# Evacuating a PSUM bank behind its last product, loading rows of x ahead, and moving row sums in a one-layer hybrid decoder kernel

## The chip, the cores and the metric

The kernel runs on one core of a Trainium2 chip. The time is device microseconds (us) of one execution of the whole program. TensorE is called PE here, VectorE DVE, ScalarE ACT, GpSimd POOL and SyncE SP; SP issues most of the transfers.

## The reference

One decoder layer in float32 on x with 512 rows and 2048 columns. Two attention groups share an input projection: A is a sliding-window attention with sinks, B a stick-breaking attention. Each group's output is RMS-normalised, both go through one output projection, and a squared-ReLU MLP of width 8192 follows:

```python
proj = rmsnorm(x, g) @ w_in                     # q_a k_a v_a q_b k_b v_b
o_a  = swa_attention(rmsnorm(q_a), rmsnorm(k_a), v_a, sinks, rel_bias)
o_b  = stick_breaking_attention(q_b, k_b, v_b)
mix  = concat([rmsnorm(o_a, swa_out_g), rmsnorm(o_b, sb_out_g)])
x    = x + mix @ w_out
u    = rmsnorm(x, norm_mlp_g) @ w_up
x    = x + square(relu(u)) @ w_down
```

The stick-breaking weights need, for each query, a running sum over the keys to its right (a scan on DVE).

## The kernel before, in words

Every float32 operand of PE is split into a high part (ACT copies it, L91) and a low part (DVE subtracts, L92), and each product is made as three matmuls (`mm3`, L113 to 118). PE's work comes in this order on the timeline of the profile:

- 0 to 140 us: load and transpose x, first projections.
- 140 to 500 us: the remaining input projections, in groups of four PSUM banks (`group_T` at L297 for q and k, `v_group` at L519 for v). Each group walks over the inner dimension in steps c; in each step it makes products into each of its four banks, and after every second bank it calls `pump()` (L276), which puts one step of an attention unit into the stream: scores z of a stick-breaking pair (L547), their weights (L560 to 572, on ACT, DVE and POOL; the scan is L567, the subtraction that reads the scores a last time is L569), and the transposes wtr of the weights (L581).
- 500 to 640 us: the first half of the output projection, `out_group(0, n)` for n of 0 to 3 (L645), on the normalised output of group B. The last stick-breaking pairs are still pumped in.
- 640 to 780 us: the second half, `out_group(1, n)`, with `evac_b` (L716) and the transposes of the new x.
- 780 to 1400 us: the up projection. For each step i, `u_load` (L762) fetches a raw weight tile, `u_sums` (L769) forms four sums of its blocks on POOL (L779), and `u_split` makes high and low parts (hi_u on ACT, lo_u on DVE); PE makes products 128x256 (L809 to 811).
- 1400 to 2041 us: the down projection (L1053 to 1055). Its weights are raw tiles (st_d) and differences of them, called T1 to T4, made on POOL by `d_sum` (L931), in two halves each; T1 of the first column is issued within the last steps of the up projection (k == 4 there).

PSUM has two pools of four banks: `pp` holds the banks of projections (ps_qk, ps_v, ps_o), `pa` scores, transposes and the sums of squares. A new tile takes the bank that comes next in rotation and waits for the last reader of what was there. Within an engine, instructions run in the order in which the program's framework places them; that order follows the order of the code with small shifts by which instruction is ready.

In the code before, a group evacuates its four banks after the loop over c: `group_T` by `evac` (L319, DVE), `v_group` by L535 on ACT, `out_group` by `evac_a` or `evac_b`. `evac_a` (L675) takes a buffer xs (tag "bias", two buffers), asks SP for 128 rows of x, adds them to the scaled bank on DVE (L678), and stores the sum. `branch_scale(b)` (L634) sums the squares S of a branch on PE with a vector of ones (rs, L637) and makes the branch's scale rb from it; `branch_scale(0)` stands before the first `out_group(0, 0)`, `branch_scale(1)` before `out_group(1, 0)`.

## Time and profile before

| quantity | value |
|---|---|
| runs | 2041.43, 2043.79 and 2044.12 us, median 2043.79 |
| profiled execution | 2043.11 us, its span 2041.0 |
| PE busy | 2004.0 us, 98% |
| DVE busy | 1626.8 us, 80% |
| POOL busy | 1020.3 us, 50% |
| ACT busy | 1014.5 us, 50% |
| DMA queue of the hardware | 345.02 MB, 49.8% of 16 engines |

The span runs from the first to the last recorded instruction; the profiled execution is 2.1 us longer. Busy time is summed over instructions, so idle time of PE is what is left, and for each idle stretch the trace names the instruction whose end released it. A granted clock of 1 means TensorE's full 2.4 GHz, 0.5 means 1.2 GHz.

### The profile page before, as it was taken

How to read it: one execution, taken by the hardware profiler on the slowest of the kernel's cores; microseconds unless marked ns; L12 is line 12 of the kernel's file. 1: busy time of each engine (PE TensorE's matmuls, PEld its weight loads, DVE VectorE, ACT ScalarE, POOL GpSimd, SP SyncE). 2: the span in 40 equal slices, each digit the busy share in tenths (PEclk: the TensorE clock that was granted, in tenths of full speed). 3: DMA queues.
4: the chain of work that ended last, by engine and by line, in shares of the span. 5: the costliest groups of instructions: out<-in, count | busy, mean ns of one | idle time of the engine just before them, and what ended most of it. 6: DMA issues, size and time to landing. Idle time of an engine off the chain costs nothing. (4 is left out here: it accounts for less than half of the span.)

```text
span 2041.0 us, 31132 instructions
## 1 busy us (share of the span) xinstructions
PE 2004.0 (98%) x11748; PEld 1725.3 (85%) x11748; DVE 1626.8 (80%) x2034; ACT 1014.5 (50%) x1676; POOL 1020.3 (50%) x904
## 2 busy tenths in 40 slices
PE   8999999999999999999999999998999999999998
PEld 7887787778677889999999999997788888888887
DVE  4378646665775578999999999998989999999987
ACT  6267534544553565555555555554543333333343
POOL 0014332222320127777777777775756556655654
PEclk9999999999999999999999999999999999999999
DMA  6742332223345555665656565656756557456351
GB/s 220 123 129 85 100 93 81 73 92 111 107 134 186 168 166 182 203 203 183 203 182 205 182 205 182 206 182 264 273 223 227 177 216 267 155 226 258 145 186 62
DMA packets 213914, 350.30 MB, mean 172 GB/s; under 512 B 9779, under 2 KB 154372, under 8 KB 206596
## 3 DMA queue, kind: packets, MB, share of 16 engines
q1 hardware_dynamic: 211216, 345.02, 49.8%
q10 hardware_dynamic: 2548, 3.30, 1.3%
q8 instruction: 92, 1.51, 0.3%
q14 instruction: 58, 0.48, 0.1%
HBM read 270.16 MB, written 78.12 MB: 171 GB/s over the span
## 5 line engine op out<-in xcount | busy, mean ns | idle before, releaser
L811 PE MATMUL ps_u<-h2h,lo_u 128*128 128x256 f32 x1824 | 515.9, 283 | 6.3 <-DVE lo_u L92 6.3
L810 PE MATMUL ps_u<-h2l,hi_u 128*128 128x256 f32 x1824 | 514.7, 282 | 2.4 <-DVE h2l L92 2.4
L809 PE MATMUL ps_u<-h2h,hi_u 128*128 128x256 f32 x1824 | 514.8, 282 | 0.1
L1053 PE MATMUL ps_d<-hi_d,ad 128*128 128x512 f32 x896 | 353.4, 394 | 3.4 <-ACT U L969 1.6
L1054 PE MATMUL ps_d<-lo_d,ad 128*128 128x512 f32 x896 | 353.4, 394 | 1.2 <-DVE lo_d L92 1.2
L1055 PE MATMUL ps_d<-hi_d,ad 128*128 128x512 f32 x896 | 353.2, 394 | 0.0
L811 PEld LDWEIGHTS ps_u<-h2h,lo_u 128*128 128x128 f32 x1824 | 346.7, 190 | 7.5 <-DVE lo_u L92 6.7
L810 PEld LDWEIGHTS ps_u<-h2l,hi_u 128*128 128x128 f32 x1824 | 346.6, 190 | 2.9 <-DVE h2l L92 2.8
L809 PEld LDWEIGHTS ps_u<-h2h,hi_u 128*128 128x128 f32 x1824 | 346.6, 190 | 0.3 <-ACT h2h L91 0.3
L779 POOL TENSOR_TENSOR s_u<-st_u 128x256 f32<-128x256 f32 (+1 forms) x256 | 200.1, 801 | 252.3 <-DVE lo_u L92 181.2
L92 DVE TENSOR_TENSOR lo_d<-T,hi_d 128x1024 fp32r<-128x1024 f32 x128 | 241.4, 1899 | 38.1 <-ACT hi_d L91 37.4
L931 POOL TENSOR_TENSOR T<-st_d,T 128x1024 f32<-128x1024 f32 x64 | 169.1, 2645 | 201.0 <-DVE lo_d L92 198.5
L91 ACT CAST hi_d<-T 128x1024 fp32r<-128x1024 f32 x128 | 134.4, 1051 | 203.0 <-PE ps_d L1055 177.6
L92 DVE TENSOR_TENSOR lo_u<-st_u,hi_u 128x384 fp32r<-128x384 f32 (+1 forms) x256 | 218.2, 853 | 4.4 <-ACT hi_u L91 4.3
L1053 PEld LDWEIGHTS ps_d<-hi_d,ad 128*128 128x128 f32 x896 | 167.9, 187 | 44.6 <-ACT U L969 2.1
L92 DVE TENSOR_TENSOR lo_d<-st_d,hi_d 128x1024 fp32r<-128x1024 f32 x96 | 193.5, 2028 | 13.7 <-ACT hi_d L91 13.2
L1054 PEld LDWEIGHTS ps_d<-lo_d,ad 128*128 128x128 f32 x896 | 168.0, 188 | 42.0 <-DVE lo_d L92 2.0
L1055 PEld LDWEIGHTS ps_d<-hi_d,ad 128*128 128x128 f32 x896 | 168.0, 187 | 40.1
L92 DVE TENSOR_TENSOR lo_u<-s_u,hi_u 128x512 fp32r<-128x512 f32 x224 | 178.1, 795 | 1.0 <-ACT hi_u L91 1.0
L91 ACT CAST hi_u<-s_u 128x512 fp32r<-128x512 f32 x224 | 138.5, 618 | 78.7 <-POOL s_u L779 78.6
L91 ACT CAST hi_d<-st_d 128x1024 fp32r<-128x1024 f32 x96 | 100.6, 1050 | 152.2 <-PE ps_d L1055 140.6
L779 POOL TENSOR_TENSOR s_u<-st_u,s_u 128x256 f32<-128x256 f32 (+1 forms) x128 | 167.8, 1311 | 10.0
(223 smaller groups left out, 3825.7 us busy)
## 6 DMA issues: line engine op xcount, KB each, us to landing
st_u<-in_w_up SPq DMA_DIRECT2D x128, 512.0 KB, 4.5
st_d<-in_w_down SPq DMA_DIRECT2D x64, 1024.0 KB, 8.3
ad<-ac SPq DMA_DIRECT2D x56, 1024.0 KB, 5.1
ac<-ah SPq DMA_DIRECT2D x32, 896.0 KB, 6.3
ac<-al SPq DMA_DIRECT2D x32, 896.0 KB, 6.6
st_qk<-in_w_in SPq DMA_DIRECT2D x64, 256.0 KB, 3.0
st_o<-in_w_out SPq DMA_DIRECT2D x32, 512.0 KB, 4.5
st_qa<-in_w_in SPq DMA_DIRECT2D x16, 512.0 KB, 4.1
```

Source lines behind the costliest of these rows:

```text
L91: nc.scalar.copy(out=hi, in_=st)
L92: nc.vector.tensor_tensor(out=lo, in0=st, in1=hi.bitcast(F32), op=ALU.subtract)
L779: nc.gpsimd.tensor_tensor(out=o, in0=a, in1=b, op=op)
L809: nc.tensor.matmul(o, wh[:, a], hh[:, b], start=first, stop=False, skip_group_check=True)
L810: nc.tensor.matmul(o, wh[:, a], hl[:, b], start=False, stop=False, skip_group_check=True)
L811: nc.tensor.matmul(o, wl[:, a], hh[:, b], start=False, stop=(k == KP - 1), skip_group_check=True)
L931: nc.gpsimd.tensor_tensor(out=o, in0=raw[cj, a, h], in1=raw[cj, b, h], op=ALU.subtract)
L1053: nc.tensor.matmul(o, al, bh[:, kk], start=first, stop=False, skip_group_check=True)
L1054: nc.tensor.matmul(o, al, bl[:, kk], start=False, stop=False, skip_group_check=True)
L1055: nc.tensor.matmul(o, ar, bh[:, kk], start=False, stop=end, skip_group_check=True)
```

## The change

Six things move. `group_T`, `v_group` and `out_group` call the evacuation directly behind a bank's last product, inside the loop. The rows of x for `evac_a` are asked for in step c2 == 2 of their group, into four buffers instead of two. `branch_scale(0)` moves into `out_group(0, 0)`, behind the second bank of step 1. `branch_scale(1)`, the end of the attention pools and the opening of the pools h2, sp and xw move into step 1 of `out_group(1, 0)`. T1 of the first column of the down projection is placed behind the last of the sums of w_up on POOL. A padding tile becomes 24 columns wide instead of 32. No engine gets another set of instructions.

```diff
     def group_T(src, name, evac, perm=None, after=None):
-        ps = [pp.tile([P, 512], F32, tag="pp", name=f"ps_{name}{m}") for m in range(4)]
+        ps, done = [pp.tile([P, 512], F32, tag="pp", name=f"ps_{name}{m}") for m in range(4)], []
...
                     mm3(ps[m], (hi[:, kk, ms], lo[:, kk, ms]), (hT[k][:, 0], hT[k][:, 1]),
                         k == 0, k == KD - 1)
+                if c == KD // 2 - 1:
+                    done.append(evac(m, ps[m]))
                 if m % 2:
                     pump()
             if after:
                 after(c)
-        return [evac(m, ps[m]) for m in range(4)]
+        return done
...
-    const.tile([P, 32], F32, name="pad_left")
+    const.tile([P, 24], F32, name="pad_left")
...
-            bias.append(wk.tile([P, 2, 2 * P], F32, tag="bias", name=f"bias{c}"))
+            bias.append(wk.tile([P, 2, 2 * P], F32, tag="bias", bufs=4, name=f"bias{c}"))
...
     def v_group(o):
...
+                if c == KD // 2 - 1:
+                    v = vp.tile([P, 512], F32, tag="v", name=f"v{o}_{t}")
+                    nc.scalar.mul(out=v, in_=ps[t], mul=r1[:, t:t + 1])
+                    vs.append(v)
                 if t % 2:
                     pump()
-        vs = []
-        for t in range(NT):
-            v = vp.tile([P, 512], F32, tag="v", name=f"v{o}_{t}")
-            nc.scalar.mul(out=v, in_=ps[t], mul=r1[:, t:t + 1])
-            vs.append(v)
         return vs
...
-    def out_group(b, n, evac, ahead=None, between=None):
+    def out_group(b, n, evac, ahead=None, between=None, within=None):
...
                     mm3(ps[t], (oc[:, 0, ts], oc[:, 1, ts]), (hi[:, kk], lo[:, kk]), c == 0, c == 7)
+                if c2 == 3:
+                    evac(n, t, ps[t])
                 if t % 2:
                     pump()
+                if within and (c2, t) == (1, 1):
+                    within()
             if between and c2 in (1, 2):
                 between(c2 - 1)
-        for t in range(NT):
-            evac(n, t, ps[t])
...
-    ra = branch_scale(0)
+    rs, xs_of = {}, {}
 
     def evac_a(n, t, ps):
-        xs = wk.tile([P, 512], F32, tag="bias", name=f"xs{n}{t}")
-        nc.sync.dma_start(out=xs, in_=xv[:, t, n * 512:(n + 1) * 512])
-        nc.vector.scalar_tensor_tensor(out=xs, in0=ps, scalar=ra[:, t:t + 1], in1=xs, op0=ALU.mult, op1=ALU.add)
+        xs = xs_of.pop(t)
+        nc.vector.scalar_tensor_tensor(out=xs, in0=ps, scalar=rs[0][:, t:t + 1], in1=xs, op0=ALU.mult, op1=ALU.add)
         nc.sync.dma_start(out=ascr[n, :, t], in_=xs)
 
+    def ahead_a(n, fetching):
+        def ahead(c2):
+            if fetching:
+                fetching(c2)
+            if c2 == 2:
+                for t in range(NT):
+                    xs_of[t] = wk.tile([P, 512], F32, tag="bias", bufs=4, name=f"xs{n}{t}")
+                    nc.sync.dma_start(out=xs_of[t], in_=xv[:, t, n * 512:(n + 1) * 512])
+        return ahead
+
+    def scale_a():
+        rs[0] = branch_scale(0)
+
     for n in range(4):
-        out_group(0, n, evac_a, fetch_two(0) if n == 0 else fetch_two(1) if n == 3 else None)
+        out_group(0, n, evac_a, within=scale_a if n == 0 else None, ahead=ahead_a(n, fetch_two(0) if n == 0 else fetch_two(1) if n == 3 else None))
     drain()
-    rb_ = branch_scale(1)
-    attn.close()
     even.close()
...
+    def begin_b(c2):
+
+        if c2 == 1:
+            rs[1] = branch_scale(1)
+            attn.close()
+            for k in range(6):
+                hp.append(mlp.enter_context(tc.tile_pool(name=f"h2_{k}", bufs=1, side="right")))
+            pools["sp"] = mlp.enter_context(tc.tile_pool(name="sp", bufs=2, side="right"))
+            pools["xw"] = tail.enter_context(tc.tile_pool(name="xw", bufs=4, side="right"))
...
-                nc.gpsimd.tensor_tensor(out=o, in0=a, in1=b, op=op)
+                last_sum[0] = nc.gpsimd.tensor_tensor(out=o, in0=a, in1=b, op=op)
...
-        out_group(1, n, evac_b, ahead=u_begin if n == 3 else None,
+        out_group(1, n, evac_b, ahead={0: begin_b, 3: u_begin}.get(n),
...
                 elif k == 4:
-                    d_sum(0, "T1")
+                    with tc.issue_after(last_sum[0].ins):
+                        d_sum(0, "T1")
```

What moves on the engines is shown at three places, the first on two engines. The rows name the output, the inputs and the shape; line numbers behind the change are larger by 2 to 22, since the file has grown.

The first is PE at the start of the first output projection. ps_o001 is the second bank of the first group, hi_o and lo_o are parts of w_out, rs0 is the sum of squares, z4_30 and z4_31 are the scores of the last block of a stick-breaking pair. Before:

```order
L116 MATMUL ps_o001_4939<-hi_o000_4944,ohl0_0_4565 128x512
L637 MATMUL rs0_4923<-ones2_494,S0_585 128x2 x4
L117 MATMUL ps_o001_4939<-lo_o000_4945,ohl0_0_4565 128x512
L118 MATMUL ps_o001_4939<-hi_o000_4944,ohl0_0_4565 128x512
L116 MATMUL ps_o001_4939<-hi_o000_4944,ohl0_1_4601 128x512
L117 MATMUL ps_o001_4939<-lo_o000_4945,ohl0_1_4601 128x512
L118 MATMUL ps_o001_4939<-hi_o000_4944,ohl0_1_4601 128x512
L547 MATMUL z4_30_4960<-hl_b22_4489,hl_b20_4479 128x512
L547 MATMUL z4_31_4961<-hl_b22_4489,hl_b20_4479 128x512
```

Behind the change, at the same place:

```order
L116 MATMUL ps_o001_4924<-hi_o000_4929,ohl0_0_4565 128x512
L117 MATMUL ps_o001_4924<-lo_o000_4930,ohl0_0_4565 128x512
L118 MATMUL ps_o001_4924<-hi_o000_4929,ohl0_0_4565 128x512
L116 MATMUL ps_o001_4924<-hi_o000_4929,ohl0_1_4601 128x512
L117 MATMUL ps_o001_4924<-lo_o000_4930,ohl0_1_4601 128x512
L118 MATMUL ps_o001_4924<-hi_o000_4929,ohl0_1_4601 128x512
L549 MATMUL z4_30_4945<-hl_b22_4483,hl_b20_4461 128x512
L549 MATMUL z4_31_4946<-hl_b22_4483,hl_b20_4461 128x512
```

rs0 has left this place, so z4_30 is the first here that takes a bank of the pool `pa`. rs0 stands one step later, behind the first scores of the next pair (z5_00 and z5_01) and ahead of the third bank:

```order
L549 MATMUL z5_00_5019<-hl_b23_4494,hl_b21_4472 128x256
L549 MATMUL z5_01_5020<-hl_b23_4494,hl_b21_4472 128x256
L639 MATMUL rs0_5053<-ones2_494,S0_585 128x2 x4
L116 MATMUL ps_o002_4925<-hi_o001_5003,ohl0_2_4637 128x512
L117 MATMUL ps_o002_4925<-lo_o001_5004,ohl0_2_4637 128x512
```

Here rs0 takes the bank behind those of z5_00 and z5_01.

On DVE at the same time, f_b is the evacuation of the last bank of a q and k group (ps_qk_3), and b4_20, a4_20, b4_21, a4_21 are the two chains of one pair whose scores lie in the banks that PE takes next. Before:

```order
L563 SCALAR_TENSOR_TENSOR b4_20_4852<-z4_20_4843,a4_20_4851 128x384
L563 SCALAR_TENSOR_TENSOR b4_21_4865<-z4_21_4844,a4_21_4864 128x384
L567 SCALAR_TENSOR_TENSOR a4_20_4851<-ones2_494,b4_20_4852 128x384
L567 SCALAR_TENSOR_TENSOR a4_21_4864<-ones2_494,b4_21_4865 128x384
L569 TENSOR_TENSOR b4_20_4852<-z4_20_4843,a4_20_4851 128x384
L569 TENSOR_TENSOR b4_21_4865<-z4_21_4844,a4_21_4864 128x384
L582 COPY wt4_0_4811<-wtr4_10_4889 128x2x128
L582 COPY wt4_1_4812<-wtr4_11_4893 128x2x128
L319 SCALAR_TENSOR_TENSOR f_b33_4917<-ps_qk3_3_4500,rbc_514 128x512
```

Behind the change:

```order
L565 SCALAR_TENSOR_TENSOR b4_20_4862<-z4_20_4853,a4_20_4861 128x384
L321 SCALAR_TENSOR_TENSOR f_b33_4904<-ps_qk3_3_4500,rbc_514 128x512
L569 SCALAR_TENSOR_TENSOR a4_20_4861<-ones2_494,b4_20_4862 128x384
L565 SCALAR_TENSOR_TENSOR b4_21_4875<-z4_21_4854,a4_21_4874 128x384
L571 TENSOR_TENSOR b4_20_4862<-z4_20_4853,a4_20_4861 128x384
L569 SCALAR_TENSOR_TENSOR a4_21_4874<-ones2_494,b4_21_4875 128x384
L584 COPY wt4_0_4811<-wtr4_10_4909 128x2x128
L571 TENSOR_TENSOR b4_21_4875<-z4_21_4854,a4_21_4874 128x384
```

The evacuation has moved from behind the chains to between them, and the first chain's subtraction (L571) now stands ahead of the second chain's scan (L569).

The second is DVE at the end of the first group of that projection, where xs are the evacuations and b_20, b_21 belong to the third block of a pair's weights. Before:

```order
L678 SCALAR_TENSOR_TENSOR xs00_5256<-ps_o000_4938,rb0_4928,xs00_5256 128x512
L678 SCALAR_TENSOR_TENSOR xs01_5260<-ps_o001_4939,rb0_4928,xs01_5260 128x512
L563 SCALAR_TENSOR_TENSOR b5_20_5211<-z5_20_5202,a5_20_5210 128x384
L563 SCALAR_TENSOR_TENSOR b5_21_5224<-z5_21_5203,a5_21_5223 128x384
L567 SCALAR_TENSOR_TENSOR a5_20_5210<-ones2_494,b5_20_5211 128x384
L567 SCALAR_TENSOR_TENSOR a5_21_5223<-ones2_494,b5_21_5224 128x384
L569 TENSOR_TENSOR b5_20_5211<-z5_20_5202,a5_20_5210 128x384
L569 TENSOR_TENSOR b5_21_5224<-z5_21_5203,a5_21_5223 128x384
L582 COPY wt5_0_5171<-wtr5_10_5248 128x2x128
L582 COPY wt5_1_5172<-wtr5_11_5252 128x2x128
L92 TENSOR_TENSOR lo_o013_5516<-st_o013_5513,hi_o013_5515 128x1024
L678 SCALAR_TENSOR_TENSOR xs02_5264<-ps_o002_4940,rb0_4928,xs02_5264 128x512
```

Behind the change:

```order
L681 SCALAR_TENSOR_TENSOR xs00_5113<-ps_o000_4923,rb0_5058,xs00_5113 128x512
L681 SCALAR_TENSOR_TENSOR xs01_5115<-ps_o001_4924,rb0_5058,xs01_5115 128x512
L681 SCALAR_TENSOR_TENSOR xs02_5117<-ps_o002_4925,rb0_5058,xs02_5117 128x512
L565 SCALAR_TENSOR_TENSOR b5_20_5223<-z5_20_5214,a5_20_5222 128x384
L565 SCALAR_TENSOR_TENSOR b5_21_5236<-z5_21_5215,a5_21_5235 128x384
L569 SCALAR_TENSOR_TENSOR a5_20_5222<-ones2_494,b5_20_5223 128x384
L569 SCALAR_TENSOR_TENSOR a5_21_5235<-ones2_494,b5_21_5236 128x384
L571 TENSOR_TENSOR b5_20_5223<-z5_20_5214,a5_20_5222 128x384
L571 TENSOR_TENSOR b5_21_5236<-z5_21_5215,a5_21_5235 128x384
L681 SCALAR_TENSOR_TENSOR xs03_5119<-ps_o003_4926,rb0_5058,xs03_5119 128x512
L584 COPY wt5_0_5179<-wtr5_10_5264 128x2x128
```

Three evacuations stand ahead of the chain of the next block where there were two, and the fourth stands directly behind it.

The third is POOL at the end of the up projection; s_u126 and s_u127 are the last sums of w_up, T1_00 and T1_01 the two halves of T1, st_d raw tiles of w_down. Before:

```order
L779 TENSOR_TENSOR s_u125_15371<-st_u125_15236,s_u125_15371 128x2x128
L931 TENSOR_TENSOR T1_00_15576<-st_d000_15477 128x1024
L779 TENSOR_TENSOR s_u126_15440<-st_u126_15303 128x2x128 x2
L779 TENSOR_TENSOR s_u126_15440<-s_u126_15440,st_u126_15303 128x2x128
L779 TENSOR_TENSOR s_u126_15440<-st_u126_15303,s_u126_15440 128x2x128
L931 TENSOR_TENSOR T1_01_15578<-st_d001_15479 128x1024
L779 TENSOR_TENSOR s_u127_15511<-st_u127_15369 128x128 x2
L779 TENSOR_TENSOR s_u127_15511<-s_u127_15511,st_u127_15369 128x128
L779 TENSOR_TENSOR s_u127_15511<-st_u127_15369,s_u127_15511 128x128
L931 TENSOR_TENSOR T3_00_15731<-st_d010_15713,st_d000_15477 128x1024
```

Behind the change:

```order
L801 TENSOR_TENSOR s_u125_15371<-st_u125_15236,s_u125_15371 128x2x128
L801 TENSOR_TENSOR s_u126_15440<-st_u126_15303 128x2x128 x2
L801 TENSOR_TENSOR s_u126_15440<-s_u126_15440,st_u126_15303 128x2x128
L801 TENSOR_TENSOR s_u126_15440<-st_u126_15303,s_u126_15440 128x2x128
L801 TENSOR_TENSOR s_u127_15511<-st_u127_15369 128x128 x2
L801 TENSOR_TENSOR s_u127_15511<-s_u127_15511,st_u127_15369 128x128
L801 TENSOR_TENSOR s_u127_15511<-st_u127_15369,s_u127_15511 128x128
L953 TENSOR_TENSOR T1_00_15576<-st_d000_15477 128x1024
L953 TENSOR_TENSOR T1_01_15578<-st_d001_15479 128x1024
L953 TENSOR_TENSOR T3_00_15731<-st_d010_15713,st_d000_15477 128x1024
```

The two halves of T1 have moved from between the sums to behind the last one.

## Rows read from the trace of the kernel before

**Rows 1.** Page, part 1: busy us (share of the span) and instructions of each engine.

```profile
PE 2004.0 (98%) x11748; PEld 1725.3 (85%) x11748; DVE 1626.8 (80%) x2034; ACT 1014.5 (50%) x1676; POOL 1020.3 (50%) x904
```

**Rows 2.** Waits of PE: line, releaser, us in total, times, longest.

```profile
PE ps_u L811 <- DVE lo_u L92: 6.3, 2, 5.4
...
PE ps_o L116 <- DVE xs L678: 4.2, 4, 1.5
...
PE wtr L581 <- ACT b L572: 2.5, 2, 1.6
...
PE z L547 <- DVE b L569: 1.2, 2, 0.6
```

**Rows 3.** Timeline of PE at 515 us: start, us, instruction [idle before, releaser].

```profile
515.86 1.05 PE L637 MATMUL rs<-ones,S 128*128 128x2 f32 x8 [3.08 <-DVE b L569]
```

**Rows 4.** Windows: length, busy of PE, PEld, DVE, ACT, POOL, clock, DMA, GB/s.

```profile
500.00:540.00 40.00, 35.99 (x178) 26.27 (x177) 28.57 (x46) 21.49 (x50) 13.29 (x21) 0.96 0.25 77
...
1398.80:1404.40 5.60, 5.60 (x26) 5.60 (x27) 4.37 (x5) 4.25 (x4) 2.38 (x1) 0.50 0.29 100
```

**Rows 5.** Timeline of PE at 619 us.

```profile
619.05 0.50 PE L116 MATMUL ps_o<-hi_o,ohl 128*128 128x512 f32 x1 [1.49 <-DVE xs L678]
```

**Rows 6.** The evacuations of L678: durations, and what DVE waited for.

```profile
L678 DVE SCALAR_TENSOR_TENSOR xs<-ps_o,rb,xs x16: 737/744/752, 545.6 to 651.8; 128x512 f32<-128x512 f32 x16
...
  DMA xs<-in_x: 5.4, 6
```

**Rows 7.** Timeline of DVE at 559 us.

```profile
559.47 1.26 DVE L569 TENSOR_TENSOR b<-z,a 128x512 f32<-128x512 f32 x2
```

**Rows 8.** Timeline of PE at 560 us.

```profile
559.93 0.39 PE L117 MATMUL ps_o<-lo_o,ohl 128*128 128x512 f32 x1
560.16 0.39 PE L118 MATMUL ps_o<-hi_o,ohl 128*128 128x512 f32 x1
560.48 0.63 PE L547 MATMUL z<-hl_b,hl_b 64*128 64x256 f32 x6
```

**Rows 9.** Timeline of DVE from 509 to 516 us.

```profile
509.39 0.69 DVE L319 SCALAR_TENSOR_TENSOR f_b<-ps_qk,rbc 128x512 f32<-128x512 f32 x1 [0.21 <-PE ps_qk L118]
...
511.16 4.19 DVE L567 TENSOR_TENSOR_SCAN a<-ones,b 128x384 f32<-128x384 f32 x2
515.28 0.99 DVE L569 TENSOR_TENSOR b<-z,a 128x384 f32<-128x384 f32 x2
```

**Rows 10.** Timeline of POOL at 511 us.

```profile
511.12 1.30 POOL L315 TENSOR_TENSOR hl_b<-f_b,hl_b 128x512 fp32r<-128x512 f32 x1
```

**Rows 11.** Timeline of DVE at 613 us, scans of that form.

```profile
613.59 2.04 DVE L567 TENSOR_TENSOR_SCAN a<-ones,b 128x384 f32<-128x384 f32 x2
```

**Rows 12.** Timeline of PE, end of the up projection.

```profile
1398.73 0.58 PE L811 MATMUL ps_u<-h2h,lo_u 128*128 128x256 f32 x1 [5.40 <-DVE lo_u L92]
```

**Rows 13.** Timeline of POOL, end of the up projection.

```profile
1378.11 2.78 POOL L931 TENSOR_TENSOR T<-st_d 128x1024 f32<-128x1024 f32 x1 [1.57 <-DVE lo_u L92]
...
1385.25 2.38 POOL L931 TENSOR_TENSOR T<-st_d 128x1024 f32<-128x1024 f32 x1
...
1390.44 2.86 POOL L931 TENSOR_TENSOR T<-st_d,st_d 128x1024 f32<-128x1024 f32 x1
1393.26 2.53 POOL L931 TENSOR_TENSOR T<-st_d,T 128x1024 f32<-128x1024 f32 x1
1395.75 2.52 POOL L931 TENSOR_TENSOR T<-st_d,st_d 128x1024 f32<-128x1024 f32 x1
```

**Rows 14.** Timeline of DVE, end of the up projection.

```profile
1391.92 1.67 DVE L836 TENSOR_TENSOR a<-a 128x256 f32<-128x256 f32 x1 [0.89 <-ACT a L834]
1393.51 2.56 DVE L839 TENSOR_TENSOR a<-a 128x256 f32<-128x256 f32 x1
1395.99 2.69 DVE L92 TENSOR_TENSOR lo_u<-st_u,hi_u 128x384 fp32r<-128x384 f32 x1
...
1399.65 0.42 DVE L840 TENSOR_TENSOR a<-a 128x256 f32<-128x256 f32 x1
```

More of the change, by code (lines that the diff above doesn't have):

```diff
@@ L521, in v_group @@
         src = cols(w_in, O5 + 512 * o)
+        vs = []
         for c in range(KD // 2):
@@ L707, in hymba_layer @@
     tail = ExitStack()
-    for k in range(6):
-        hp.append(mlp.enter_context(tc.tile_pool(name=f"h2_{k}", bufs=1, side="right")))
-    sp = mlp.enter_context(tc.tile_pool(name="sp", bufs=2, side="right"))
-    xw = tail.enter_context(tc.tile_pool(name="xw", bufs=4, side="right"))
+    pools = {}
+    def begin_b(c2):
[6 more added lines that the diff above has]
+            pools["xw"] = tail.enter_context(tc.tile_pool(name="xw", bufs=4, side="right"))
     h2 = {}
@@ L716, in evac_b @@
     def evac_b(n, t, ps):
-        xt = xw.tile([P, 512], F32, tag="xt", name=f"x2_{n}{t}")
+        xt = pools["xw"].tile([P, 512], F32, tag="xt", name=f"x2_{n}{t}")
         nc.sync.dma_start(out=xt, in_=ascr[n, :, t])
-        nc.vector.scalar_tensor_tensor(out=xt, in0=ps, scalar=rb_[:, t:t + 1], in1=xt, op0=ALU.mult, op1=ALU.add)
+        nc.vector.scalar_tensor_tensor(out=xt, in0=ps, scalar=rs[1][:, t:t + 1], in1=xt, op0=ALU.mult, op1=ALU.add)
         nc.sync.dma_start(out=x2scr[n, :, t], in_=xt)
-        xs = xw.tile([P, 512], F32, tag="xs", bufs=8, name=f"xs2_{n}{t}")
+        xs = pools["xw"].tile([P, 512], F32, tag="xs", bufs=8, name=f"xs2_{n}{t}")
         nc.scalar.activation(out=xs, in_=xt, func=AF.Square, accum_out=ss2[:, t, n:n + 1])
@@ L739, in turn_x2 @@
         k = 2 * n + kk
-        hq = xw.tile([P, 8, HP], F32, tag="hq", bufs=1, name=f"hq{k}")
+        hq = pools["xw"].tile([P, 8, HP], F32, tag="hq", bufs=1, name=f"hq{k}")
         for r in range(2):
@@ L759, in hymba_layer @@
     wu = w_up.rearrange("(k p) c -> p k c", p=P)
-    raws, sums, parts_u = {}, {}, {}
+    raws, sums, parts_u, last_sum = {}, {}, {}, [None]
     def u_load(i):
@@ L771, in u_sums @@
             w = raws[i]
-            s_ = sp.tile([P, 2, 4, P], F32, tag="s", name=f"s_u{i}")
+            s_ = pools["sp"].tile([P, 2, 4, P], F32, tag="s", name=f"s_u{i}")
             if i % (KP // 2) == PLAIN // 2:
```

## The prediction

> **What bounds the kernel now.** I read the busy shares of the page first: PE is busy for 2004.0 of 2041.0 us [rows 1]. The change removes no product, so it can win idle time of PE or time at the low TensorE clock, nothing else. Next I read the list of what PE waited for [rows 2]. Five of its lines lie where the change moves something: the banks of the first out projection that wait for their evacuation on DVE (L678), 4.2 us in four waits; the transposes of the stick-breaking weights (wtr, L581) that wait for ACT, 2.5 in two; the low parts of w_up at the end of the up projection (lo_u, L92), 6.3 in two; and the scores z, 1.2 in two; the row sums of squares (rs, L637) are the fifth, one wait of 3.08 [rows 3]. Third, the windows [rows 4]. In 500 to 540 us the granted clock is 0.96 of full speed (600 to 640, around the longest xs wait, has the same 0.96), and 40 x 0.04 = 1.6 us of full-speed work is lost in each; from 1398.8 to 1404.4 it is 0.50, that is 1.2 instead of 2.4 GHz, so 5.6 x 0.5 = 2.8 us are lost. Last, the timelines around each wait; they come with the parts below.
>
> The bound is therefore PE in order, and each gap stands for one late tile of another engine.
>
> **First out projection, evacuations (xs).** The longest of the four waits is the 1.49 us in front of 619.05 [rows 5]: the next group's first product needs a bank that DVE has not read yet. One evacuation takes 0.744 us, sixteen of them together waited 5.4 us for x rows still in flight [rows 6], because the old code asks for a row when it evacuates. The change asks for the four rows half a group earlier and evacuates a bank behind its last product, while PE still has up to three banks of six products to make. Both causes go, so 4.2 us is the upper end of the gain. What is late next are the scores: DVE now does three evacuations ahead of the next pair's weights where it did two, and that chain gives back the two banks that the next scores take. Its last subtractions run to 559.47 + 1.26 = 560.73, and PE starts the next scores at 560.48 [rows 7, 8]: no slack for one more evacuation of 0.744. The nearest price is the z line of [rows 2], 0.6 each; I take two of them, 1.2, with ends of 0 and 4.2 (every wait moves from xs to z). Net **3.0**.
>
> **Sums of squares later (rs0).** Before, PE stands 3.08 us in front of 515.86 because rs0 takes the bank of a score whose subtraction on DVE (L569) is late [rows 3]. DVE is late since its two scans took 4.19 us [rows 9], while POOL subtracted in SBUF at 511.12 [rows 10]; the same two scans elsewhere take 2.04 [rows 11]. Moving rs0 does not free a bank: z4_30 and z4_31 now take that bank and the next one. PE arrives five products later, 5 x 0.23 = 1.15 us (two products in a row start at 559.93 and 560.16 [rows 8]). The second bank needs the second subtraction, half of 0.99 later, and DVE's order now has an evacuation of 0.69 between the two chains [rows 9]. With scans as slow as before the wait is 3.08 - 1.15 + 0.50 + 0.69 = 3.1, no gain; with scans at 2.04 it is 2.15 less, 1.0. The gain lies between 0 and 2.1; I take the middle, **1.0**. In its new place rs0 stands behind the scores z5_0 and takes whichever bank is next; its 8 products of 128x2 are short, and the scale is wanted first by an evacuation two steps of c2 later, so I cost it at nothing; if that cover were gone, PE would wait the length of the small chain behind it once.
>
> **The other evacuations.** Those of q, k and v also move ahead of up to two pumped attention steps. That can help a transposition (wtr, 2.5 us waited at present) or delay a chain by one evacuation of 0.69 [rows 2, 9]. Where a chain is tight now, around 180 and 345 us, two places could each lose one: ends 0 and -1.4, taken **-0.9**; for wtr ends 0 and 2.5, taken **0.4**, since nothing in its own chain gets shorter.
>
> **Low clock.** Both 1.6 us losses follow a PE wait that the change attacks: 3.08 us before 515.86 and 1.49 us before 619.05 [rows 3, 5]. The second wait should go; the first shrinks. Ends 0 and 3.2; I take both, **3.2**, the second being the surer.
>
> **Second branch scale, pools, pads.** rs1 moves into the first group of the second projection, where it is needed only by that group's evacuations; none of the listed waits is for it, so 0. The later pools hold tiles first used at the same evacuations: 0. The additional loads on SP pass one weight load of w_out per group; no wait of PE in [rows 2] is for the w_out weights, so that cover is wide. evac_b moves nowhere on DVE, so its 0.
>
> **Up to down projection (T1 behind the last sums).** PE's largest wait, 5.40 us before 1398.73 [rows 12], ends with a lo_u. The four T pieces on POOL from 1390.44 on are back to back for three of them [rows 13], and each covers one DVE instruction with both operands in SBUF: L836, L839 and lo_u take 1.67, 2.56 and 2.69, while the same form as L839 takes 0.42 with POOL quiet (L840, 1399.65) [rows 14]. So three T pieces, not the sums of w_up, hold DVE. The change takes the two halves of T1, 2.78 and 2.38, from between the sums and puts them behind the last: the sums end up to 5.16 earlier, T1 then takes 5.16, and T3 starts at 1390.44 again. The same three pieces meet the same three DVE instructions: **0**, with ends of -9.1 (below: C) and +9.6 (E). The Trainium skill (page "SBUF — State Buffer", section "Who interferes with whom") says that a VectorE instruction with two SBUF inputs and a GpSimd instruction that reads SBUF exclude each other for a whole instruction, by which started first. The rows just named agree; by that rule this edit moves the exclusion and removes none, so it speaks against the gain in C, and the sum stays at 0 for this part.
>
> **The sum.** 3.0 + 1.0 - 0.9 + 0.4 + 3.2 + 0 = 6.7 us. The profiled execution took 2043.11 us, 2.1 us more than its span; the runs' median is 2043.79, so it stands 0.7 above the profiled one, inside the runs' spread of 2.7. 2043.1 - 6.7 = **2036.4**.
>
> **Rivals.**
> A, the forecast: 2036.4. Its own bounds: all gains full (4.2 + 2.1 + 2.5 + 3.2 = 12.0) is not plausible at once; with 4.2 + 2.1 + 0.4 + 3.2 and no loss it is 2033.2. Chance 0.48.
> B, the wait in front of the first out projection stays at z4 (scans still slowed by POOL) and keeps its low clock: 1.0 + 1.6 less, 2039.0. For it: the bank order, and POOL's subtractions stand in the same place; against it: one chain no longer waits for both scans. Chance 0.20.
> C, T1 out of the way of the sums lets every lo_u come in time: 6.3 and 2.8 us more, 2027.3. For it: T1 delays two of the sums now; against it: the three later pieces stay where they are [rows 13, 14]. Chance 0.12.
> D, the change moves order but no wait goes: the xs waits reappear at z, 4.2 against 4.2, the low clocks stay, and the 0.4 and 1.0 cancel most of 0.9: 2043.1 - 0.6 = 2042.5. For it: no slack at 560.48. Chance 0.12.
> E, slower: the last sums cannot start earlier because their raw tiles' buffers or DVE's earlier lo_u hold them, so T1 is simply added in front of T3. It decides once T3 starts about 5 us after 1390.44. PE's wait grows by 5.2, the sixth piece can hold one more lo_u for up to 2.4, of which I take 1.7 since that one is needed some products later, and the low stretch grows in the proportion 5.6 to 5.4 at half speed, 2.7: 9.6 us on top, 2046.0, slower than before. For it: six pieces in one row have no gap for DVE; against it: the sums do stand behind T1 now. Chance 0.08.
>
> **How the numbers follow.** A is likeliest, so 2036.4. A, B and D together hold 0.80; from A's lower bound, and half of C's gain (2036.4 - 4.6 = 2031.8) since the pieces might let go in part, to D with the 0.7 between profile and median: 2031.5 to 2043. C in full and E are left out. A measurement of this kernel can tell about 0.2%, 4.1 us, so faster means under 2039.7: nearly all of A (0.45), a little over half of B (0.11) and C (0.12), 0.68. Slower means over 2047.9: E with other small losses, and a low-clock stretch in a place I don't see, 0.05. The rest, 0.27, is no change.
>
> **What would show it.** Right: no xs wait over 0.3 us, z waits of 0.5 to 0.7 in at most two of the next scores, the window 600 to 640 at clock 1.00, z4_30 the first waiter after 510 us with 1 to 3 us, and a lo_u wait still near 5 us, T3 starting at the same distance from the end of the last sums' products. Wrong: xs waits that persist because DVE is behind with the chain (then the x rows were not the cause); a low clock at a place where it was full before; a lo_u wait under 2 us (C) or near 10 (E).

## The result: faster by 0.9%, nearly three times the forecast

The changed kernel takes 2024.45 us (median of four runs, 2023.99 to 2026.89) against 2043.39 for the kernel before on the same chip. The ratio is 0.9911, with a 95% interval of 0.9894 to 0.9928. The forecast was 2036.4 with a range of 2031.5 to 2043: the sign was right, the size was not, and the time lies below the range.

Where the 18.9 us came from is seen by cutting both profiled executions at PE's first product of the up projection (ps_u) and of the down projection (ps_d), and at the last product of the latter, read from PE's timeline:

| stretch | before, us | after, us | difference | forecast |
|---|---|---|---|---|
| start to first ps_u | 740.9 | 735.1 | -5.8 | -6.7 |
| up projection | 665.7 | 664.4 | -1.3 | 0 |
| down projection | 630.7 | 619.0 | -11.7 | 0 |

In this pair of executions the part that the forecast worked out came nearly as said, and two thirds of the gain lie in a stage in which no instruction moved except T1 at its very start. The first line is partly luck: the changed kernel's three stretches were 735.7, 662.2 and 622.3 us in a repetition (after_again, below), and the first took 739.7 us in t1_between, whose program differs only behind it. The page of the changed kernel gives one hint. The shares of busy time are within a point of those before [rows 1], but PE is busy for 13.5 us less with the same 11748 instructions:

```profile
PE 1990.5 (98%) x11748; PEld 1729.3 (86%) x11748; DVE 1609.5 (80%) x2034; ACT 1017.5 (50%) x1676; POOL 1021.4 (51%) x904
```

The list of PE's waits is the answer to [rows 2] (columns as there). The line of xs is gone and the two waits for wtr are shorter. PE's scores z and its products with lo_d (the low parts of w_down) wait more, and a wait for f_q, an evacuation of a group of q_a, is new:

```profile
PE ps_d L1077 <- DVE lo_d L92: 3.8, 3, 2.1
PE z L549 <- DVE b L571: 3.6, 6, 0.7
PE ps_u L833 <- DVE lo_u L92: 2.6, 1, 2.6
...
PE z L549 <- DVE wt L584: 1.5, 2, 0.8
PE ps_qa L116 <- DVE f_q L321: 1.2, 1, 1.2
...
PE wtr L583 <- ACT b L574: 1.0, 2, 0.8
```

Windows answer [rows 4] (length, busy time and count of PE, PEld, DVE, ACT, POOL, then clock, DMA share, GB/s). Both stretches that were at 0.96 are at full clock, and one that was at 1.00 is not (the last line; the kernel before has 1.00 there):

```profile
500.00:540.00 40.00, 38.37 (x195) 28.57 (x194) 28.53 (x50) 23.98 (x56) 14.13 (x23) 1.00 0.25 80
...
600.00:640.00 40.00, 39.87 (x192) 30.63 (x191) 30.37 (x46) 20.69 (x38) 7.77 (x14) 1.00 0.49 156
...
340.00:360.00 20.00, 17.71 (x82) 12.51 (x81) 15.74 (x26) 9.41 (x21) 5.99 (x12) 0.91 0.18 54
```

None of this explains the down projection. What does is PE's pace in stretches where it never waits. Two windows, one in the middle of the up projection and one in the middle of the down projection; first the kernel before:

```profile
800.00:1100.00 300.00, 300.00 (x2529) 300.00 (x2528) 272.56 (x368) 170.58 (x281) 224.13 (x235) 1.00 0.61 200
1500.00:1900.00 400.00, 400.00 (x1723) 322.69 (x1722) 374.43 (x303) 150.88 (x144) 239.46 (x83) 1.00 0.55 205
```

then the changed kernel:

```profile
800.00:1100.00 300.00, 300.00 (x2502) 300.00 (x2501) 262.80 (x369) 169.86 (x278) 224.10 (x236) 1.00 0.61 198
1500.00:1900.00 400.00, 400.00 (x1766) 331.20 (x1766) 385.07 (x312) 156.40 (x149) 238.24 (x83) 1.00 0.57 212
```

PE is busy for all of each window and the clock is 1.00 in all four. In 400 us of the down projection PE starts 1723 products before and 1766 after: 232.2 ns for one against 226.5. In 300 us of the up projection it is the other way round, 2529 against 2502, 118.6 ns against 119.9. Each instruction has become quicker or slower by itself, with the same shape and at the same clock.

Only one line of the change reaches all of these instructions: the padding tile `pad_left`, 24 columns instead of 32. Every tile behind it on the left side of SBUF starts 32 bytes earlier. A product has two operands in SBUF, the weights (their loads are PEld in the profile) and the moving operand of 512 or 256 columns. The table joins, for each product, the start bytes of the two modulo 64 (the remainder of the address divided by 64, from the program's layout) with the mean time to the next product's start (from the trace, without the products behind a wait or at low clock and without a few that are more than 20 ns late; with the late ones the first row is 118.8 and the fifth 120.1):

```
kernel   products            moving starts at   weights start at   count   mean ns
before   up, 128x256         0                  32                 4008    118.3
before   up, 128x256         32                 32                 1406    119.9
before   down, 128x512       32                 0                  2295    233.3
before   down, 128x512       32                 32                 383     227.1
after    up, 128x256         0                  0                  5462    120.0
after    down, 128x512       0                  0                  2671    226.7
```

For 128x512 products, different starts cost 6.6 ns each; for 128x256 products, different starts save 1.7 ns. Within the kernel before the two groups of the down projection run side by side, with 233.3 and 227.1 ns, so this is no difference between two executions or two chips. The fast group uses one of the seven kinds of activation tile; in the changed kernel its products and those of the other six all take 226.7 to 226.9. The 128x512 products of the first stretch have equal starts in both kernels and keep their pace (ps_qa: 227.4 and 227.6 ns). The estimate from it: 2295 x 6.6 ns = 15 us less in the down projection, 4008 x 1.7 = 7 us more in the up projection (5 with the late ones).

### The profile page after: what moved, and what is told of

It reads as the page before. It is cut to its first block, busy times and chain, and to the rows that moved or that the text cites. A ratio compares the mean times of both kernels' runs of the same rounds, so it can differ in the third digit from the quotient of the medians.

```text
span 2022.2 us, 31123 instructions
## 1 busy us (share of the span) xinstructions
PE 1990.5 (98%) x11748; PEld 1729.3 (86%) x11748; DVE 1609.5 (80%) x2034; ACT 1017.5 (50%) x1676; POOL 1021.4 (51%) x904
## 5 line engine op out<-in xcount | busy, mean ns | idle before, releaser
L1076 PE MATMUL ps_d<-hi_d,ad 128*128 128x512 f32 x896 | 349.3, 390 | 2.8 <-ACT U L991 1.6
L1078 PE MATMUL ps_d<-hi_d,ad 128*128 128x512 f32 x896 | 349.2, 390 | 0.0
L92 DVE TENSOR_TENSOR lo_d<-T,hi_d 128x1024 fp32r<-128x1024 f32 x128 | 245.9, 1935 | 27.4 <-ACT hi_d L91 26.7
L91 ACT CAST hi_u<-st_u 128x384 fp32r<-128x384 f32 (+1 forms) x256 | 134.0, 524 | 221.5 <-PE ps_u L832 131.4
L92 DVE TENSOR_TENSOR lo_u<-st_u,hi_u 128x384 fp32r<-128x384 f32 (+1 forms) x256 | 200.5, 784 | 19.9 <-ACT hi_u L91 19.9
```

The lines of the kernel that those rows point to most:

```text
L91: nc.scalar.copy(out=hi, in_=st)
L92: nc.vector.tensor_tensor(out=lo, in0=st, in1=hi.bitcast(F32), op=ALU.subtract)
L1076: nc.tensor.matmul(o, al, bh[:, kk], start=first, stop=False, skip_group_check=True)
L1078: nc.tensor.matmul(o, ar, bh[:, kk], start=False, stop=end, skip_group_check=True)
```

## The experiments

Theory L: the layout gives most of the gain, and the moves about what was forecast. Rival S: the moves did it all. Each ratio is to the kernel before on the same chip.

**The moves without the layout.**

```diff
-    const.tile([P, 24], F32, name="pad_left")
+    const.tile([P, 32], F32, name="pad_left")
```

> The changed kernel with the padding tile put back to 32 columns, so that every tile of the left side starts 32 bytes further, where it stood before the change; all moves stay. Theory L (the layout is most of the gain): the 2304 down products whose moving operand starts at 32 and whose weights start at 0 modulo 64 bytes go back from 226.7 to 233.4 ns, 15.4 us, and the 4032 up products with the moving operand at 0 and weights at 32 from 120.1 to 118.8, 5.2 us less: about 2034.5 us, between 2032 and 2037. Rival S (the moves did it all): 2024.5, down products at 226.7 ns.

Measured: 2039.79 us, ratio 0.9985 (0.9976 to 0.9994). The windows of this kernel have the counts of the kernel before:

```profile
800.00:1100.00 300.00, 300.00 (x2529) 300.00 (x2528) 272.07 (x370) 170.78 (x280) 223.28 (x237) 1.00 0.61 201
1500.00:1900.00 400.00, 400.00 (x1723) 322.66 (x1722) 374.60 (x305) 150.43 (x144) 236.29 (x82) 1.00 0.56 205
```

The moves alone are worth about 3 us (1.2 to 4.9 by the interval), the direction of the forecast and less than half of its 6.7. The time is above the range that theory L gave (2032 to 2037), because L counted 5.2 us for the up projection's quicker pace, and a wait took them back: PE waits 5.93 us once for lo_u here, against 2.64 in the changed kernel, and the up projection lasts 665.4 us, 1 more than there. In the first stretch a wait for f_q of 2.9 us, which the kernel before doesn't have, takes back as much of the gain (below, the bias loads).

**The layout without the moves.** The kernel before with this one edit:

```diff
-    const.tile([P, 32], F32, name="pad_left")
+    const.tile([P, 24], F32, name="pad_left")
```

> The kernel before with nothing changed but the padding tile, 24 columns instead of 32. Theory L: down products at 226.7 ns instead of 233.4, up products at 120 instead of 118.8: about 10 us faster than before, 2033, with the PE waits for xs (four, up to 1.5 us), rs (3.1) and lo_u still there. Rival S: the same time as before, 2043.4.

Measured: 2033.21 us, ratio 0.9947 (0.9935 to 0.9960): 9.7 us from eight columns of a tile that nobody reads. Its window in the down projection:

```profile
1500.00:1900.00 400.00, 400.00 (x1766) 331.22 (x1765) 385.97 (x312) 156.39 (x149) 245.05 (x84) 1.00 0.56 210
```

The waits for xs (4.4 us in four) and rs (3.1) are still there, as theory L said. S has fallen. The two parts add up to 12.8 us, where both together gave 18.9 in the first comparison and 14.3 in a second one (after_again, below); the intervals of these ratios are 4 to 7 us wide each, so I don't claim an interaction from times alone.

**Different starts in the down projection alone.** The activation tiles, which are the weights of these products on PE, start 8 elements further in their buffers:

```diff
-            a = (aba if i == ORDER[0] else abb).tile([P, 2, 4, HP], F32R, tag="a", name=f"ad{c}{i}")
+            a = (aba if i == ORDER[0] else abb).tile([P, 8 + 8 * HP], F32R, tag="a", name=f"ad{c}{i}")[:, 8:].rearrange("p (a k t) -> p a k t", a=2, k=4)
```

> The changed kernel, but the activation tiles of the down projection (its weights on PE) start 32 bytes further in their buffers; 1536 of 2688 products then have the moving operand at 0 and the weights at 32 modulo 64 bytes. If what slows a 128x512 product is any difference between the two starts: 233 ns for these, 10 us slower than the changed kernel. If it is the moving operand alone that must not start at 32 while the weights start at 0, and the opposite case is the faster one, as in the up projection: 224 to 225 ns, 3 to 4 us faster.

Measured: 2037.59 us, ratio 0.9975 (0.9964 to 0.9985), 9 us slower than the yardstick beside it:

```profile
1500.00:1900.00 400.00, 400.00 (x1725) 323.64 (x1724) 374.82 (x305) 151.57 (x144) 232.39 (x82) 1.00 0.56 208
```

By the joined table, 1525 products with the moving operand at 0 and weights at 32 take 233.4 ns. So weights 32 further cost the same as a moving operand 32 further for 128x512. The longer buffers also spread the other tiles over several multiples of 64 bytes; those 1146 products take 230.4 ns on average, not 226.7. Joined modulo 256 instead, with the moving operand at 0, they are three groups: weights at 0 take 228.6 ns, at 192 229.4, and at 128 233.2, as slow as the odd multiples of 32 (233.0 to 233.9). So equal starts modulo 64 are not the rule. In the kernel before and in the changed one every pair that is equal modulo 64 is also equal modulo 256, so those two can't tell. As a by-product h2 tiles of two steps moved to 32 with weights at 0, and their 1428 up products take 117.9 ns: for 128x256 too, the sign doesn't matter.

**Different starts in the up projection alone.**

```diff
-            hi = whl.tile([P, 7, P], F32R, tag="hi", name=f"hi_u{i}")
+            hi = whl.tile([P, 8 + 7 * P], F32R, tag="hi", name=f"hi_u{i}")[:, 8:].rearrange("p (a c) -> p a c", a=7)
...
```

> The changed kernel, but the high and low parts of w_up start 8 elements (32 bytes) further inside their buffers; nothing else moves. Theory L2 (the start of weights against that of the moving operand sets the pace of a product): all 5472 up products at 118.8 instead of 120.1 ns, 7 us less work for PE, of which the waits at the end of the up projection give some back: 2018 to 2022. Rival: the pace of 118.8 in the kernel before had another cause: 2024.5 and 120.1 ns.

Measured: 2027.68 us, ratio 0.9917 (0.9903 to 0.9931), no gain. The pace is there, 118.3 ns, and the wait at the end has taken it back; its window, and its line in the list of PE's waits:

```profile
800.00:1100.00 300.00, 300.00 (x2531) 299.45 (x2530) 272.01 (x370) 169.68 (x280) 223.27 (x236) 1.00 0.61 201
```

```profile
PE ps_u L833 <- DVE lo_u L92: 6.3, 2, 5.9
```

The wait for lo_u is 6.3 us instead of 2.6, and the clock is low behind it (0.93 from 1370 to 1420 us, against 0.97). The up projection lasts 665.3 us against 664.4. With T on POOL as here, its end is set by DVE's work under POOL's, not by PE's pace. That is also why the slower pace of the up projection cost little in the other direction: before_pad24's lasts 666.1 us, the kernel before's 665.7.

**T1 back between the sums.**

```diff
-                    with tc.issue_after(last_sum[0].ins):
-                        d_sum(0, "T1")
+                    d_sum(0, "T1")
```

> The changed kernel with T1 put back between the last sums of w_up. Theory N (what was forecast: that part is worth nothing): 2024.5, the lo_u wait at the end of the up projection within 1 us of 2.6. Rival G (T1's new place lets the later T pieces start earlier against PE): the wait goes back to between 4 and 6 us, with a longer stretch at low clock, 2026.5 to 2030.

Measured: 2027.38 us, ratio 0.9921 (0.9908 to 0.9933). The time lies within G's, but the changed kernel itself took 2028.29 in the next comparison (below), so the times don't decide. The waits do: those for lo_u and lo_d at the end of the up projection are 3.45 and 0.64 us here, 2.64 and 2.13 in the changed kernel, and 0.49 and 4.30 in its repetition. The sums are 4.1, 4.8 and 4.8, and G's 4 to 6 us for lo_u did not come. The loss moves between two waits, as much between two executions of one kernel as by the place of T1, so N stands. The additional time of the profiled execution lies ahead of T1: its first stretch took 739.7 us, and the clock was low for 6.8 us at 108.6 and for 3.4 at 521.6.

**The yardstick once more.** The changed kernel, unchanged, in the next comparison:

> The changed kernel itself once more, as the yardstick for the three runs beside it: 2024.5 us, between 2023 and 2027, with a wait for an evacuation of the second q_a group near 108 us of 1.2 to 3.0 us.

Measured: 2028.29 us, ratio 0.9926 (0.9914 to 0.9939), a little over the range that I had given. The two ratios of the same kernel overlap; a difference of 2 or 3 us between runs of different comparisons is not evidence here, so below I lean on waits that come and go.

**The bias loads.** The wait for f_q near 108 us (1.2 us here, 1.9 in the repetition, 2.4 to 3.0 in the five other kernels with the wider buffer, none in the kernel before and in before_pad24) was in nobody's forecast. The wider bias buffer (four instead of two) lets SP issue twice as many bias loads ahead of the weights of q_a. SP's timeline in the kernel before, then in the changed one (start, us, issues):

```profile
95.52 1.76 SPq L425 DMA_DIRECT2D bias<-skew  x4
```

```profile
94.20 3.66 SPq L427 DMA_DIRECT2D bias<-skew  x8
```

The edit gives the rows of x four buffers of their own behind the weight load of their step, and the bias tiles two again:

```diff
-            bias.append(wk.tile([P, 2, 2 * P], F32, tag="bias", bufs=4, name=f"bias{c}"))
+            bias.append(wk.tile([P, 2, 2 * P], F32, tag="bias", name=f"bias{c}"))
...
-                    xs_of[t] = wk.tile([P, 512], F32, tag="bias", bufs=4, name=f"xs{n}{t}")
-                    nc.sync.dma_start(out=xs_of[t], in_=xv[:, t, n * 512:(n + 1) * 512])
+                    xs_of[t] = wk.tile([P, 512], F32, tag="xs", bufs=4, name=f"xs{n}{t}")
+                    with tc.issue_after(last_load[0].ins):
+                        nc.sync.dma_start(out=xs_of[t], in_=xv[:, t, n * 512:(n + 1) * 512])
```

> The changed kernel, but the bias tiles keep two buffers and the rows of x get four of their own, asked for behind the weight load of the same step; only the order of transfers on SP differs. Theory B (the four additional bias loads ahead of the q_a weights, which the wider buffer lets start early, make those weights land late): no PE wait near 108 us, the longest st_qa landing back from 6 to 8 us to about 4.4, and 1.2 to 4 us less than the changed kernel. Rival: that wait comes from the evacuations' new order on DVE: the same wait, the same time.

Measured: 2023.97 us, ratio 0.9909 (0.9895 to 0.9922), 4.3 less than the repetition beside it; the two intervals just overlap, so the wait decides. It is gone. The line on how long the loads of st_qa, the weights of q_a, take to land, in the changed kernel and then in this one:

```profile
DMA to landing us min/median/max: 3.5/3.7/5.9
```

```profile
DMA to landing us min/median/max: 3.7/3.9/4.4
```

The longest load is at 4.4 us again, as in the kernel before (3.7/4.1/4.4). Theory B holds.

**The T pieces of the first column left out.**

```diff
+                if cj == 0 and name != "T4":
+                    raw[cj, name, h] = raw[cj, a, h]
+                    continue
```

> The changed kernel without T1, T2 and T3 of the first column of the down projection (the raw tile is used in their place; this part of the output is left out). Theory H (T pieces on POOL hold DVE instructions with two operands in SBUF): L859, L862 and the last lo_u near 0.42 to 0.7 us each, no PE wait over 1 us for lo_u at the end of the up projection, none over 1 for lo_d behind it, full clock there: 4 to 6.5 us less than the changed kernel. Rival D (DVE is late with its own work there): the wait stays over 2 us, less than 1 us gained.

Measured: 2022.24 us, ratio 0.9901 (0.9887 to 0.9914), 6.0 less than the repetition beside it. The up and the down projection take 661.5 and 617.3 us, against 662.2 and 622.3 there. DVE's timeline in the changed kernel, then in this one, for the same three instructions:

```profile
1388.73 2.62 DVE L859 TENSOR_TENSOR a<-a 128x256 f32<-128x256 f32 x1
1391.38 2.50 DVE L862 TENSOR_TENSOR a<-a 128x256 f32<-128x256 f32 x1
1393.81 2.84 DVE L92 TENSOR_TENSOR lo_u<-st_u,hi_u 128x512 fp32r<-128x512 f32 x1
```

```profile
1389.45 0.42 DVE L859 TENSOR_TENSOR a<-a 128x256 f32<-128x256 f32 x1
1389.91 0.43 DVE L862 TENSOR_TENSOR a<-a 128x256 f32<-128x256 f32 x1
1390.28 0.69 DVE L92 TENSOR_TENSOR lo_u<-st_u,hi_u 128x512 fp32r<-128x512 f32 x1
```

2.62, 2.50 and 2.84 us become 0.42, 0.43 and 0.69, and PE's list of waits has no line for lo_u any more. Theory H holds, and with it the forecast's reading of [rows 13, 14]. On POOL, in the changed kernel, the last three pieces lie nearly exactly over the three long instructions:

```profile
1381.42 5.09 POOL L953 TENSOR_TENSOR T<-st_d 128x1024 f32<-128x1024 f32 x2
1388.65 2.42 POOL L953 TENSOR_TENSOR T<-st_d,st_d 128x1024 f32<-128x1024 f32 x1 [2.13 <-DMA st_d<-in_w_down]
1391.02 2.58 POOL L953 TENSOR_TENSOR T<-st_d,T 128x1024 f32<-128x1024 f32 x1
1393.56 2.54 POOL L953 TENSOR_TENSOR T<-st_d,st_d 128x1024 f32<-128x1024 f32 x1
```

This is what the Trainium skill says in "SBUF — State Buffer", section "Who interferes with whom": a VectorE instruction with two SBUF inputs and a GpSimd instruction that reads SBUF shut each other out for a whole instruction. The trace agrees, 2.62 us beside a piece and 0.42 without one.

**The first column's T2 and T3 on DVE**, on top of bias_two:

```diff
-                nc.gpsimd.tensor_tensor(out=o, in0=raw[cj, a, h], in1=raw[cj, b, h], op=ALU.subtract)
+                (nc.vector if cj == 0 and name in ("T2", "T3") else nc.gpsimd).tensor_tensor(
+                    out=o, in0=raw[cj, a, h], in1=raw[cj, b, h], op=ALU.subtract)
```

> The kernel with two bias buffers (bias_two) and, for the first column of the down projection, T2 and T3 on DVE behind the last lo_u instead of on POOL. Theory H (the T pieces on POOL hold DVE's two-operand instructions): no PE wait over 1 us for lo_u at the end of the up projection; DVE gets four subtractions of about 1.2 us each behind it, so a wait for lo_d of 2 to 4 us may stay: 1.5 to 4 us less than bias_two, 2020 to 2022.5. Rival: DVE's additional work comes back as a longer lo_d wait: within 1 us of bias_two, 2024.

Measured: 2020.99 us, ratio 0.9889 (0.9876 to 0.9903). No wait for lo_u remains; DVE's later work is waited for instead, 1.74 us for an e (L851, a sum ahead of the ReLU) at 1403.92. The time is 3.0 us less than that of bias_two, which ran in another comparison. In the profiled executions the up projection is 2.9 us shorter (661.5) and the down projection 1.0 longer (620.0); the rest lies in the first stretch, which the edit does not touch.

**All three edits**, the up projection's different starts added:

> As bias_two_t_dve, and the parts of w_up 32 bytes further in their buffers, so that all up products have different starts modulo 64 bytes and all down products the same. Theory: up products at 118.3 instead of 120.0 ns; what the wait at the end of the up projection took back in up_weights32 is now gone, so 5472 x 1.7 ns = 9 us, less 2 to 4 us that DVE's pace takes back: 2014 to 2018. Rival (the up projection is bound by DVE as soon as PE is faster): 2020 or more.

Measured: 2017.21 us, ratio 0.9871 (0.9858 to 0.9885). The up projection lasts 657.0 us instead of 661.5, and the down projection 621.2 instead of 620.0, because PE comes earlier to the same work of DVE:

```profile
1399.58 0.77 PE L1078 MATMUL ps_d<-hi_d,ad 128*128 128x512 f32 x1 [3.08 <-DVE e L846]
```

This kernel beats both; 26 us against the kernel before, 7 against the changed one by the first comparison, 11 by the ratio of the second.

**rs0 back in front**, on top of bias_two:

```diff
+    rs[0] = branch_scale(0)
...
-        out_group(0, n, evac_a, within=scale_a if n == 0 else None, ahead=ahead_a(n, fetch_two(0) if n == 0 else fetch_two(1) if n == 3 else None))
+        out_group(0, n, evac_a, ahead=ahead_a(n, fetch_two(0) if n == 0 else fetch_two(1) if n == 3 else None))
```

> bias_two with the sums of squares rs0 put back in front, where they stood before the change; all else as in bias_two. By the forecast's part on rs0: a PE wait of about 3 us for DVE b at 514 us and 1.6 us of low clock behind it, where bias_two waits 1.3 us in two: 2 to 4 us slower, 2026 to 2028. Rival (the order of the evacuation between the two chains on DVE is what shortens the wait, not rs0): the wait below 2 us, 2024 to 2025.

Measured: 2025.30 us, ratio 0.9912 (0.9898 to 0.9925). PE waits 1.23 us for rs0, not 3; but the window behind it is at low clock, where bias_two's is at 1.00:

```profile
515.95 1.05 PE L639 MATMUL rs<-ones,S 128*128 128x2 f32 x8 [1.23 <-DVE b L571]
```

```profile
500.00:520.00 20.00, 18.77 (x90) 13.68 (x89) 15.74 (x26) 11.69 (x26) 7.53 (x11) 0.93 0.18 54
```

So neither expectation holds whole. The wait fell from 3.08 [rows 3] to 1.23 with rs0 in its old place, and moving rs0 gained nothing more (0.54 + 0.77 in the changed kernel). The layout is not the cause either: before_pad24 waits 3.05. The new order on DVE is what is left, and its two scans fit: 4.19 us together before [rows 9], 2.05 and 0.96 in the changed kernel:

```profile
513.04 2.05 DVE L569 TENSOR_TENSOR_SCAN a<-ones,b 128x384 f32<-128x384 f32 x1
...
516.00 0.96 DVE L569 TENSOR_TENSOR_SCAN a<-ones,b 128x384 f32<-128x384 f32 x1
```

Here they take 2.04 and 0.96. The low clock cost 20 x 0.07 = 1.4 us. That it came from rs0's place is not shown: in t1_between rs0 stands in its new place, PE waits 0.55 and 0.78 us, and the clock of 520 to 540 us is 0.91.

**The rows of x late**, the evacuations behind their products as in the change:

```diff
...
-        xs = xs_of.pop(t)
+        xs = wk.tile([P, 512], F32, tag="bias", name=f"xs{n}{t}")
+        nc.sync.dma_start(out=xs, in_=xv[:, t, n * 512:(n + 1) * 512])
...
```

> The changed kernel with two buffers for bias and rows of x, and the rows asked for when a bank is evacuated, as before the change; the evacuations stay directly behind the last products. If the late rows of x are what made PE wait for xs: four waits for xs of 0.7 to 1.5 us again, 2 to 5 us slower than bias_two, 2026 to 2029. If it was the place of the evacuation behind the loop: no xs wait over 0.3 us, 2024 to 2025.

Measured: 2025.91 us, ratio 0.9918 (0.9905 to 0.9932). PE's waits:

```profile
PE ps_o L116 <- DVE xs L682: 4.2, 4, 1.3
...
PE z L549 <- DVE b L571: 2.5, 4, 0.7
```

All 4.2 us of xs waits are back, as in [rows 2]. The late rows were the cause; evacuating behind the product does nothing for these waits alone. The z waits are 2.5 us in four instead of 3.6 in six.

## Why the prediction was wrong, step by step

**The step that failed is "Second branch scale, pools, pads ... 0".** The padding tile stands in the heading and gets no sentence of its own: I took bytes that nobody reads for free. It was worth 9.7 us alone (0.9947), more than all moves together. Every product of PE has its operands at the addresses of this layout, and the forecast's opening rule, that a change which removes no product can win only idle time or low clock, left out a third thing: the time of one product. The kernel before had the evidence in it: the same 128x512 form at 233 and at 227 ns between starts within one stage. I looked at waits and at the clock, and never at the distance between starts in a stretch without waits.

Of the 15 us that the layout gives in the down projection, about 3.5 came back: PE's idle time there rose from 4.6 to 6.5 us, and the low clock behind the wait for lo_d at 1401.96 took about 1.6:

```profile
1396.70 0.38 PE L833 MATMUL ps_u<-h2h,lo_u 128*128 128x256 f32 x1 [2.64 <-DVE lo_u L92]
...
1401.96 0.80 PE L1077 MATMUL ps_d<-lo_d,ad 128*128 128x512 f32 x1 [2.13 <-DVE lo_d L92]
```

The sum of the moves was too high as well: 6.7 us against the 3.1 of moves_pad32. In the first comparison the first stretch hid this, with a gain of 5.8 in one pair of executions. Of the signs named, three came: no xs wait over 0.3 us, two z waits near 0.55, the full clock from 600 to 640 us. Two did not: a z4_30 wait of 1 to 3 us (0.54) and a lo_u wait near 5 (2.64). One sign of being wrong came, a low clock at a place where it was full (340 to 360 us).

**First out projection, xs: 3.0 forecast, 3.1 measured.** The 4.2 us are gone, and two new z waits of 0.56 and 0.55 came at 558 and 591 us, as many as were priced and a little cheaper than 0.6. x_rows_late shows that the cause was the one named.

**Sums of squares: 1.0 forecast, 1.8 measured.** The wait of 3.08 [rows 3] became 0.54 for z4 and 0.77 for the copy behind it. The two scans took 3.0 us, between the forecast's 4.19 and 2.04. rs_early shows that the fall does not come from moving rs0; DVE's new order, which the forecast had counted as a cost of 0.69, is what is left.

**Low clock: 3.2 forecast, 3.2 measured** in these two windows (0.96 to 1.00 twice), but 20 x 0.09 = 1.8 us were lost anew from 340 to 360 us, behind two z waits of 0.66 and 0.77. Net that is 1.4, less than half of the term. The repetition has the same two waits there and a clock of 1.00, so a part of this term is chance from one execution to the next.

**The other evacuations: -0.9 and +0.4 forecast.** The wtr waits fell from 2.5 to 1.0 us, 1.5 gained. New are z waits of 0.66 and 0.77 near 342 us, 0.6 for a product of the q norm, and the 1.2 for f_q, about 3.3 lost, so -1.8 for the -0.5 of the two terms. The last wait was mis-sized for a reason that the forecast did not look at: "the additional loads on SP" were costed at the out projection, and the four bias loads that the wider buffer lets start at 94 us were missed. bias_two shows it.

**Up to down projection: 0 forecast, rightly.** In moves_pad32, with the layout of before, the wait for lo_u is 5.93 us against 5.40 [rows 12]; t1_between differs from the changed kernel only in where the loss stands. The wait of 2.64 in the changed kernel does not come from T1's place: PE makes its products 1.7 ns slower each and arrives later at the same wait, as in before_pad24, where T1 stands in its old place and the wait is 3.45. no_t_first confirms the mechanism on which the 0 stood. Rival C, that the sums were what held lo_u, has fallen, and E did not happen.

**Range and rivals.** All rivals were about waits in PE's order. None was about the pace of PE, so a range over all of them could not hold the time. (In D, 0.4 + 1.0 - 0.9 is 0.5 and not 0.6; nothing hangs on it.)

What stays open: why a 128x512 product is slower and a 128x256 product faster when its operands start 32 bytes apart, what rule of the starts holds in general (128 bytes apart modulo 256 cost as much in ad_weights32, 233.2 ns), and why the clock falls behind the same waits in one execution and not in another.

## What to carry to other kernels

Before costing waits, divide a stretch without waits by its number of products, in each stage and for each operand tile: two paces of one form in one trace are time that no wait shows. Treat every change of a tile's size, pads included, as a change of all addresses behind it, and check PE's pace again after it. A wider buffer is also an earlier transfer: look for what then stands in the queue behind it.

## What the runs showed of the hardware

- At a granted clock of 1.00, a 128x512 float32r product of the down projection took 226.7 to 227.1 ns from start to start with both operands at the same start modulo 256 bytes (the kernel before and the changed one) and 233.3 with starts 32 apart, whichever operand was shifted. With other distances, in ad_weights32, it took 228.6 (none), 229.4 (192) and 233.2 ns (128). A 128x256 product took 120.0 with equal starts and 117.9 to 118.3 ns with starts 32 apart, the other way round.
- PE's pace in the up projection did not set the end of that stage: 118.3 instead of 120.0 ns changed its length from 664.4 to 665.3 us as long as POOL's T pieces held DVE, and from 661.5 to 657.0 once T2 and T3 were off POOL.
- A wait of 1.23 us was followed by a low clock in rs_early, while waits of 1.10 and 1.27 us in x_rows_late were not (no window below 1.00 between 500 and 735 us there). Behind the same two waits of 0.66 and 0.77 us near 342 us the clock of 340 to 360 us was 0.91 in the changed kernel and 1.00 in its repetition. The length of a wait alone does not tell.
